# Where the attention output is split into 16-bit halves: at its making, or at its use by the output projection

## Chip, cores and metric

One core of one Trainium2 chip. The metric is the device time of one execution in microseconds (us); lower is better. TensorE is PE, VectorE DVE, ScalarE ACT, GpSimd POOL, and SyncE, which issues nearly all transfers, SP.

## The reference

Two layers over 16 meta tokens and 2048 frames of width 1024. Layer 0 (a linear recurrence and a state-space branch) isn't touched. Layer 1 is stick-breaking attention with 16 heads of 64, a gate, an output projection and a residual; a norm follows, and the meta tokens are dropped:

```
u = rmsnorm(h, norm_w)
q, k, v, g = split(u @ w_in, 4)
z = einsum('bthd,bshd->bhts', q, k) * 64 ** -0.5
log_keep = where(before, log_sigmoid(-z), 0)            # before: key index < query index
csum = cumsum(log_keep, axis=-1)
weights = where(before, exp(log_sigmoid(z) + csum[..., -1:] - csum), 0)
o = einsum('bhts,bshd->bthd', weights, v)
o = o * silu(g)
h = h + o @ w_out
return rmsnorm(h, final_norm)[:, 16:]
```

## The kernel before

Every product in float32 precision is made of three products of 16-bit halves (`mm3`, lines 395 to 397): each operand is written as a high and a low half, and high x high, high x low and low x high are summed.

**Stages.** Layer 0 fills the time to about 1400 us. Layer 1 follows and is written by a planner: `build_proj(p)` and `build_attn(p)` for eight pairs of heads, and `build_out()` at last, only list operations with an engine, a duration, a priority and the buffers they use. `Planner.run` lays them out once, always taking the operation that can start first by its own durations and, among those, the one of the smallest priority number. The order per engine is then fixed in the program: each engine runs its list from the front and waits at whatever isn't ready.

**Projection of a pair** (`build_proj`): keys, values, queries and gate, in chunks of up to 512 columns, each chunk 24 matmuls. The gate lands in `sg`, four buffers, one per 512 queries (L1875 on ACT, L1878 on DVE). The value path has a split of its own into halves: ACT copies to 16 bits (L1789), DVE subtracts (L1792), from SBUF to SBUF.

**Attention of a pair** (`build_attn`): four blocks `i` of 512 queries. For each block the key blocks go from the diagonal one down to the meta tokens. A *score step* is 128 queries against up to 512 keys for two heads: four matmuls into `zp` (L1911, two buffers), a sigmoid on ACT (L1934), two scans on DVE (L1939 on the diagonal, widths 128, 256, 384 and 512; L1942 elsewhere, width 512), a copy to 16 bits on ACT (L1946), the low half on POOL (L1949), and a transposing transfer into `tb` on SP (L1953). Four score steps make a *value step*: 24 matmuls into `op` (L1986). A block ends with a meta score step (16 narrow matmuls, scan L2010) and a meta matmul (L2032). Then its output is made: DVE scales it and adds a term into `og` (L2040), POOL multiplies it by the gate (L2043), and SP stores it as float32 into `o_d` (L2046): 32 such blocks, 8 pairs by 4.

**Output projection** (`build_out`): 16 tiles of 128 tokens, O0 to O15. A tile's load from `o_d` needs the block of all eight pairs, so O0 to O3 need the last pair's first block, O4 to O7 its second. The weights of `w_out` are split on ACT and DVE (L2104, L2107). For each tile SP loads float32 into `wraw` (two buffers, L2131), ACT makes the high half (L2134) and DVE the low half (L2137) in `ohl`, PE runs 48 matmuls in two column halves, DVE adds the residual (L2157), ACT squares and sums (L2161), and the norm follows (L2168 to L2177) with the store. The first six tiles share one `ohl` buffer, `first`; the later ones go round four.

Of the kernel before, what the change touches and what calls it, by code (L numbers as in the profile page):

```python
# [8 lines left out]
F32 = mybir.dt.float32  # L9
F32R = mybir.dt.float32r  # L10
F16 = mybir.dt.float16
I32 = mybir.dt.int32
U16 = mybir.dt.uint16
AF = mybir.ActivationFunctionType
# [5 lines left out]
P = 128  # L20
D = 1024
KT = 8
# [241 lines left out]
def trunk_kernel(ctx: ExitStack, tc: tile.TileContext, a: dict, out: bass.AP, stop=None):  # L264
# [26 lines left out]
    wz_d = dram.tile([3, P, 2, KT, 256], F16, name="wz_d")  # L291
    ac_d = dram.tile([HEADS, NT, P], F32, name="ac_d")
    h1_d = dram.tile([L, D], F32, name="h1_d")
    o_d = dram.tile([P, KT, SEQ], F32, name="o_d")

    ident = const.tile([P, P], F32, name="ident")
    make_identity(nc, ident)
# [1395 lines left out]
    def act_t(n, psum=True, ap=False):  # L1693
        return n * 0.000833 + 0.2 + (0.03 if ap else 0.0)

    def dve_t(n, ap=False):
        return n * 0.00104 + 0.068 + (0.06 if ap else 0.0)
# [187 lines left out]
    def build_attn(p):  # L1885
# [107 lines left out]
        def mstep(ui, prio):  # L1993
# [48 lines left out]
            def fg():  # L2042
                G.tensor_tensor(out=og.t, in0=og.t, in1=sg.t, op=ALU.mult)  # L2043

            def fd():
                nc.sync.dma_start(out=o_d[:, p, 512 * i:512 * i + 512], in_=og.t)  # L2046
            sd.op("V", dve_t(512), fo, r=[op, (vt, 0), (vt, 1), (vt, i + 1)], w=[og], prio=prio + PV_LAG)
            sd.op("G", gp_t(512), fg, r=[sg], w=[og], prio=prio + PV_LAG)
            sd.op(SP, DMA_T - 0.1, fd, r=[og], w=[(od_b, (p, i))], prio=prio + PV_LAG, lat=2.5)

        for ui, u in enumerate(units):
            t0 = start[ui]
# [13 lines left out]

    def build_out():
        base = TP * 8 + D_OFF
        oform = ("ohl", [P, 2, KT, P], F16)
        w1 = [sd.buf("u%d" % c, ("w1", [P, 2, 2, D], F16)) for c in range(4)]  # L2070
        w1r = sd.buf("vv", ("w1r", [P, 2, D], F32))
        slots = [(sd.buf("wraw", ("w1s", [P, 1, D], F32)), 0) for _ in range(6)] + [(w1r, 0), (w1r, 1)]
# [7 lines left out]
        def f1():  # L2080
            V.tensor_tensor(out=w1c[:, 0:KT], in0=osc, in1=w1m, op=ALU.mult)
            V.tensor_reduce(out=w1c[:, KT:KT + 1], in_=w1c[:, 0:KT], op=ALU.max, axis=AX.X)

        def f2():
            T.matmul(psc.t[:, 0:1], ones, w1c[:, KT:KT + 1], start=True, stop=True)
# [11 lines left out]
        for k, (b, o) in enumerate(slots):  # L2097
# [5 lines left out]
            def fh(k=k, b=b, o=o):  # L2103
                S.activation(out=wv(0, k), in_=b.t[:, o], func=AF.Copy, scale=w1c[:, k:k + 1])  # L2104

            def fl(k=k, b=b, o=o):
                V.scalar_tensor_tensor(out=wv(1, k), in0=b.t[:, o], scalar=w1c[:, k:k + 1], in1=wv(0, k),  # L2107
                                       op0=ALU.mult, op1=ALU.subtract)
# [11 lines left out]
        rest = [sd.buf(x, oform) for x in ("kk", "vv", "vv")] + [first]  # L2120
        for t in range(SEQ // P):
            pr = base - 50 + 11 * t
            raw, ohl = sd.buf("wraw"), first if t < D_TWO else rest[(t - D_TWO) % 4]
            hb, jk = [sd.buf(x, ("h1" + x, [P, 512], F32)) for x in ("whi", "wlo")], sd.buf("og", ("junk", [P, 2, 512], F16))
            st = {}

            def o3(ohl, i):
                return ohl.t[:, i]

            def ld1(t=t, raw=raw):  # L2130
                nc.sync.dma_start(out=raw.t, in_=o_d[:, :, P * t:P * t + P])  # L2131

            def fh(raw=raw, ohl=ohl):
                S.activation(out=o3(ohl, 0), in_=raw.t, func=AF.Copy)  # L2134

            def fl(raw=raw, ohl=ohl):
                V.tensor_tensor(out=o3(ohl, 1), in0=raw.t, in1=o3(ohl, 0), op=ALU.subtract)  # L2137
            sd.op(SP, DMA_T - 0.1, ld1, r=[(od_b, (p, t // 4)) for p in range(8)], w=[raw], prio=pr - 30, lat=3.5, rank=pr)
            for h in range(2):
                def ld2(t=t, b=hb[h], h=h):  # L2140
                    nc.sync.dma_start(out=b.t, in_=h1_d[NM + P * t:NM + P * t + P, 512 * h:512 * h + 512])
                sd.op(SP, DMA_T - 0.1, ld2, w=[hb[h]], prio=pr - 20, lat=3.0, rank=pr)
            sd.op("S", 0.95, fh, r=[raw], w=[(ohl, 0)], prio=pr - EVAC, rank=pr)
            sd.op("V", 1.13, fl, r=[raw, (ohl, 0)], w=[(ohl, 1)], prio=pr - EVAC)
            for h in range(2):
                hs = slice(512 * h, 512 * h + 512)
                ps = sd.buf("acc")
                for s0 in range(0, KT, 2):
                    def f(s0=s0, ps=ps, hs=hs, ohl=ohl):
                        mm3(ps.t, (lambda k: o3(ohl, 0)[:, s0 + k, :], lambda k: o3(ohl, 1)[:, s0 + k, :]),  # L2150
                            (lambda k: wv(0, s0 + k)[:, hs], lambda k: wv(1, s0 + k)[:, hs]), 2,
                            start=s0 == 0, stop=s0 == KT - 2)
                    sd.op("T", mmt(512, 6), f, w=[ps], prio=pr + D_MM + 5 * h + s0 * 0.5,
                          r=[(ohl, 0), (ohl, 1)] + [(w1[s0 // 2], (x, s0 + k)) for x in range(2) for k in range(2)])

                def fa(ps=ps, b=hb[h]):
                    V.scalar_tensor_tensor(out=b.t, in0=ps.t, scalar=w1c[:, KT + 1:KT + 2], in1=b.t, op0=ALU.mult, op1=ALU.add)  # L2157

                def fq(b=hb[h], jk=jk, h=h, st=st):
                    st["ss%d" % h] = small.tile([P, 1], F32, name="sse%d" % h)  # L2160
                    S.activation(out=jk.t[:, h], in_=b.t, func=AF.Square,  # L2161
                                 accum_out=st["ss%d" % h])
                sd.op("V", dve_t(512), fa, r=[ps], w=[hb[h]], prio=pr + 6 + 5 * h - EVAC)
                oq = sd.op("S", 0.6, fq, r=[hb[h]], w=[(jk, h)], prio=pr + 6 + 5 * h - EVAC)
# [56 lines left out]
```

## Time and profile before

| what | us |
|---|---|
| median of three runs (lowest, highest) | 2712.23 (2711.01, 2716.89) |
| the profiled execution | 2712.38 |
| its span | 2710.6 |
| PE busy in the span | 2618.6 (97%) |
| DVE busy | 2076.7 (77%) |
| ACT busy | 1645.0 (61%) |
| POOL busy | 1237.7 (46%) |

The span is what the trace covers; the execution's own time is 1.8 us longer. Times in the trace count from the span's start. A matmul's listed duration overlaps that of the next one, so what one costs is read from start to start. The granted clock of PE is given as a share of full speed: 1.00 is 2.4 GHz, and 0.5 would be 1.2 GHz.

### The profile page before, as it was taken

How to read it: one execution, taken by the hardware profiler on the slowest of the kernel's cores; microseconds unless marked ns; L12 is line 12 of the kernel's file. 1: busy time of each engine (PE TensorE's matmuls, PEld its weight loads, DVE VectorE, ACT ScalarE, POOL GpSimd, SP SyncE). 2: the span in 40 equal slices, each digit the busy share in tenths (PEclk: the TensorE clock that was granted, in tenths of full speed). 3: DMA queues.
4: the chain of work that ended last, by engine and by line, in shares of the span. 5: the costliest groups of instructions: out<-in, count | busy, mean ns of one | idle time of the engine just before them, and what ended most of it. 6: DMA issues, size and time to landing. Idle time of an engine off the chain costs nothing. (4 is left out here: it accounts for less than half of the span.)

```text
span 2710.6 us, 44621 instructions
## 1 busy us (share of the span) xinstructions
PE 2618.6 (97%) x16597; PEld 1406.4 (52%) x16597; DVE 2076.7 (77%) x2945; ACT 1645.0 (61%) x2516; POOL 1237.7 (46%) x1256
## 2 busy tenths in 40 slices
PE   7999999987999999999999999999999999999998
PEld 5765656564655555554454444444444444443344
DVE  8887786878564877689846888888888888888953
ACT  7756647456554666576625666676666666666621
POOL 4100100011203455456615776777676777766610
PEclk9999999998998999999999999999999999999999
DMA  8111111654325687888845788788787887789862
GB/s 226 53 51 55 32 55 47 196 189 136 115 98 131 176 194 177 192 184 180 182 103 118 164 175 169 171 161 175 154 179 162 169 173 163 178 170 221 211 186 101
DMA packets 974716, 404.87 MB, mean 149 GB/s; under 512 B 804017, under 2 KB 935681, under 8 KB 972834
## 3 DMA queue, kind: packets, MB, share of 16 engines
q1 hardware_dynamic: 967760, 385.39, 60.9%
q0 software_dynamic: 4640, 16.59, 1.6%
q8 instruction: 130, 2.13, 0.3%
q14 instruction: 88, 0.72, 0.1%
q10 hardware_dynamic: 2098, 0.05, 0.0%
HBM read 144.66 MB, written 60.22 MB: 76 GB/s over the span
## 5 line engine op out<-in xcount | busy, mean ns | idle before, releaser
L395 PE MATMUL acc<-u,whi 128*128 128x512 f16 (+4 forms) x2336 | 801.7, 344 | 2.9 <-DVE jk L670 1.5
L396 PE MATMUL acc<-u,whi 128*128 128x512 f16 (+4 forms) x2336 | 799.4, 343 | 2.4 <-DVE u L705 2.4
L397 PE MATMUL acc<-u,wlo 128*128 128x512 f16 (+4 forms) x2336 | 799.2, 343 | 0.0
L1949 POOL TENSOR_TENSOR hl<-e,hl 128x1024 f16<-128x1024 f32 (+2 forms) x320 | 602.5, 1886 | 187.1 <-ACT hl L1946 179.2
L1942 DVE TENSOR_TENSOR_SCAN e<-zp,carry,zero 128x512 f32<-128x512 f32 x384 | 470.6, 1267 | 47.4 <-ACT zp L1934 17.2
L1934 ACT ACTIVATE zp<-zp,ncz 128x1024 f32<-128x1024 f32 (+2 forms) x320 | 304.6, 956 | 197.4 <-PE zp L1911 166.0
L395 PEld LDWEIGHTS <-whi 128*128 128x128 f16 x2336 | 232.4, 99 | 208.6 <-issue 45.1
L1946 ACT ACTIVATE hl<-e 128x1024 f16<-128x1024 f32 (+2 forms) x320 | 293.9, 922 | 61.1 <-DVE e L1942 22.0
L397 PEld LDWEIGHTS <-wlo 128*128 128x128 f16 x2336 | 229.6, 98 | 195.1 <-issue 3.1
L396 PEld LDWEIGHTS <-whi 128*128 128x128 f16 x2336 | 229.8, 98 | 165.4 <-issue 2.4
L1911 PE MATMUL zp<-kk,qt 64*128 64x512 f16 (+9 forms) x1792 | 276.2, 301 | 7.5 <-DVE e L1939 4.5
L1939 DVE TENSOR_TENSOR_SCAN e<-zp,onehot 128x128 f32<-128x128 f32 (+3 forms) x256 | 195.6, 807 | 70.0 <-ACT zp L1934 33.4
L1911 PEld LDWEIGHTS <-qt 128*128 128x128 f16 (+1 forms) x1792 | 97.8, 95 | 192.1 <-issue 119.7
L1986 PE MATMUL op<-tb,vv 128*64 128x512 f16 (+3 forms) x1920 | 193.6, 351 | 0.5 <-DMA tb<-hl 0.2
L1986 PEld LDWEIGHTS <-vv 128*64 128x64 f16 x1920 | 101.0, 110 | 91.4 <-issue 27.8
L481 DVE SCALAR_TENSOR_TENSOR cv<-xin,scv,cv 128x512 f32<-128x512 f32 (+2 forms) x180 | 122.5, 695 | 10.6 <-ACT cv L479 8.3
L363 POOL TENSOR_TENSOR wraw<-wraw,gain 128x2048 f32<-128x2048 f32 (+1 forms) x9 | 33.4, 3706 | 172.0 <-DMA wraw<-in_even_w_in_dram 172.0
L1333 ACT ACTIVATE acr<-acr,act 128x128 f32<-128x128 f32 (+1 forms) x272 | 84.8, 382 | 38.8 <-DMA acr<-ac_d 36.9
L771 DVE SCALAR_TENSOR_TENSOR lx<-xin,prm,lx 128x512 f32<-128x512 f32 (+5 forms) x144 | 96.9, 679 | 11.3 <-ACT lx L757 7.7
L397 PE MATMUL acc<-w,ohl 128*128 128x512 f16 x256 | 98.3, 384 | 4.7 <-DVE ohl L2137 4.7
L395 PE MATMUL ops<-woh,ya 128*128 128x512 f16 x256 | 99.5, 389 | 0.4 <-DVE mb L978 0.3
L543 POOL TENSOR_TENSOR wraw<-wraw,gain 128x2048 f32<-128x2048 f32 x8 | 30.5, 3816 | 151.8 <-DMA wraw<-in_even_w_in_dram 134.7
(376 smaller groups left out, 5025.5 us busy)
## 6 DMA issues: line engine op xcount, KB each, us to landing
wraw<-in_even_w_in_dram SPq DMA_DIRECT2D x17, 1024.0 KB, 5.3
wr<-in_even_w_out_dram SPq DMA_DIRECT2D x32, 512.0 KB, 4.2
acr<-ac_d SPq DMA_DIRECT2D x64, 256.0 KB, 4.3
wraw<-in_odd_w_in_dram SPq DMA_DIRECT2D x30, 512.0 KB, 5.1
xh_d<-hw SPq DMA_DIRECT2D x20, 516.0 KB, 3.3
wz<-wz_d SPq DMA_DIRECT2D x9, 1024.0 KB, 5.4
ya_d<-ri POOLq DMA_DIRECT2D x16, 516.0 KB, 3.0
xt<-in_x_dram SPq DMA_DIRECT2D x16, 512.0 KB, 5.2
```

The lines of the kernel that those rows point to most:

```text
L395: T.matmul(ps, lh(k), rh(k), start=start and k == 0, stop=False)
L396: T.matmul(ps, lh(k), rl(k), start=False, stop=False)
L397: T.matmul(ps, ll(k), rh(k), start=False, stop=stop and k == nk - 1)
L481: V.scalar_tensor_tensor(out=dst[:, c0:c0 + n], in0=xin[:, j:j + n], scalar=wv[:, j:j + 1], in1=dst[:, c0:c0 + n], op0=ALU.mult, op1=ALU.add)
L771: V.scalar_tensor_tensor(out=lx.t[:, c0:c0 + n], in0=xin.t[:, q:q + n], scalar=prm[:, kt, q:q + 1], in1=lx.t[:, c0:c0 + n], op0=ALU.mult, ...
L1911: T.matmul(zp(hd), qt[rs, 2 if tl == ROWS else hd, P * j:P * j + P], k[rs, hd, ks], start=tl == order[0] and x == 0, stop=tl == order[1] a ...
L1934: S.activation(out=zp.t[:, :, :wd], in_=zp.t[:, :, :wd], func=AF.Sigmoid, scale=scl["ncz"])
L1939: V.tensor_tensor_scan(out=er, data0=kr, data1=onehot[:, 512 - wd:][:, ::-1], initial=0.0, op0=ALU.mult, op1=ALU.max)
L1942: V.tensor_tensor_scan(out=er, data0=kr, data1=zero.to_broadcast([P, wd]), initial=cin.t[:, 2 * j + hd:2 * j + hd + 1], op0=ALU.mult, op1= ...
L1946: S.activation(out=hlv()[:, :, 0], in_=ev(), func=AF.Copy)
L1949: (V if vl else G).tensor_tensor(out=hlv()[:, :, 1], in0=ev(), in1=hlv()[:, :, 0], op=ALU.subtract)
L1986: T.matmul(op.t[64 * hd:64 * hd + 64, c0:], vv.t[:, v0 + m, vi, 64 * hd:64 * hd + 64], tb.t[:, m, 2 * hd + wi, c0:], start=diag and m == 0 ...
```

## The change

`o_d` holds 16-bit halves instead of float32, in the same number of bytes: per partition and block of 128 tokens first the high, then the low half. The halves are made where the block's output is made: after POOL's gate product ACT copies `og` to 16 bits and DVE subtracts, both into the gate's buffer `sg`, whose bytes are free by then; SP stores from there. The output projection loads halves straight into `ohl`, and its two conversion passes per tile are gone. O0 to O5 now use the two `wraw` buffers as `ohl`, in place of the one `first`.

```
-    o_d = dram.tile([P, KT, SEQ], F32, name="o_d")
+    o_d = dram.tile([P, KT, SEQ // P, 2, P], F16, name="o_d")
...
+            o4 = lambda: og.t.rearrange("p (m c) -> p m c", c=P)
+            oh = lambda: sg.t.bitcast(F16).rearrange("p (m s c) -> p m s c", s=2, c=P)
+            def f1():
+                S.activation(out=oh()[:, :, 0], in_=o4(), func=AF.Copy)
+            def f2():
+                V.tensor_tensor(out=oh()[:, :, 1], in0=o4(), in1=oh()[:, :, 0], op=ALU.subtract)
             def fd():
-                nc.sync.dma_start(out=o_d[:, p, 512 * i:512 * i + 512], in_=og.t)
+                nc.sync.dma_start(out=o_d[:, p, 4 * i:4 * i + 4], in_=oh())
...
-            sd.op(SP, DMA_T - 0.1, fd, r=[og], w=[(od_b, (p, i))], prio=prio + PV_LAG, lat=2.5)
+            sd.op("S", act_t(512, psum=False), f1, r=[og], w=[sg], prio=prio + PV_LAG)
+            sd.op("V", dve_t(512), f2, r=[og], w=[sg], prio=prio + PV_LAG)
+            sd.op(SP, DMA_T - 0.1, fd, r=[sg], w=[(od_b, (p, i))], prio=prio + PV_LAG, lat=2.5)
...
-            raw, ohl = sd.buf("wraw"), first if t < D_TWO else rest[(t - D_TWO) % 4]
+            ohl = sd.buf("wraw", oform) if t < D_TWO else rest[(t - D_TWO) % 4]
...
-                nc.sync.dma_start(out=raw.t, in_=o_d[:, :, P * t:P * t + P])
+                nc.sync.dma_start(out=ohl.t, in_=o_d[:, :, t])
...
-            sd.op("S", 0.95, fh, r=[raw], w=[(ohl, 0)], prio=pr - EVAC, rank=pr)
-            sd.op("V", 1.13, fl, r=[raw, (ohl, 0)], w=[(ohl, 1)], prio=pr - EVAC)
```

Since the planner lays all of layer 1 out anew, the order of every engine changes from the first pair on. Two places matter for what follows. The first is DVE after the last gate chunk of the last pair (`sg<-acc`; scans stand as SCALAR_TENSOR_TENSOR with `e` as output; L2119 in the changed kernel is L2107 before, L2161 is L2157, and L2053 is the new subtraction). Before:

```order
L1878 SCALAR_TENSOR_TENSOR sg<-acc,co,sg 128x512
L1939 SCALAR_TENSOR_TENSOR e<-zp,onehot 128x384 x2
L2107 SCALAR_TENSOR_TENSOR w_26697<-w1r,w1c,w_26697 128x1024
L2137 TENSOR_TENSOR ohl<-wraw,ohl 128x1024
L1939 SCALAR_TENSOR_TENSOR e<-zp,onehot 128x512 x2
L2107 SCALAR_TENSOR_TENSOR w_26697<-w1r,w1c,w_26697 128x1024
L2040 SCALAR_TENSOR_TENSOR og<-op,vt 128x512
L1942 SCALAR_TENSOR_TENSOR e<-zp,carry,zero 128x512 x5
L2157 SCALAR_TENSOR_TENSOR h1whi<-acc,w1c,h1whi 128x512
```

And now:

```order
L1939 SCALAR_TENSOR_TENSOR e<-zp,onehot 128x256 x2
L2119 SCALAR_TENSOR_TENSOR w_26529<-w1r,w1c,w_26529 128x1024
L1939 SCALAR_TENSOR_TENSOR e<-zp,onehot 128x384 x2
L2119 SCALAR_TENSOR_TENSOR w_26529<-w1r,w1c,w_26529 128x1024
L1878 SCALAR_TENSOR_TENSOR sg<-acc,co,sg 128x512
L1939 SCALAR_TENSOR_TENSOR e<-zp,onehot 128x512 x2
L2040 SCALAR_TENSOR_TENSOR og<-op,vt 128x512
L1942 SCALAR_TENSOR_TENSOR e<-zp,carry,zero 128x512 x2
L2053 TENSOR_TENSOR sg<-og,sg 128x4x128
L1942 SCALAR_TENSOR_TENSOR e<-zp,carry,zero 128x512 x6
L1939 SCALAR_TENSOR_TENSOR e<-zp,onehot 128x128 x2
```

From the last gate chunk to the first residual add of O0 (L2157) stood five single scans of L1942; now eight stand there, and a further diagonal set begins before it.

The second place is SP around the store of the last pair's block and the first loads for the output projection (`tb<-hl` are the transposes, `o_d` the stores and loads). Before, the store and what follows it:

```order
L2046 DMA o_d<-og 128x512
L2101 DMA w1s<-in_odd_w_out_dram 128x1024
L1953 DMA_TRANSPOSE tb<-hl 128x16x128
L2101 DMA w1s<-in_odd_w_out_dram 128x1024
L1953 DMA_TRANSPOSE tb<-hl 128x16x128 x2
L2131 DMA wraw<-o_d 128x8x128 x2
L2141 DMA h1whi<-h_d 128x512
```

And now:

```order
L1953 DMA_TRANSPOSE tb<-hl 128x12x128
L2056 DMA o_d<-sg 128x1024
L1953 DMA_TRANSPOSE tb<-hl 128x16x128 x2
L2130 DMA sg<-in_final_norm_dram 128x512
L2143 DMA ohl<-o_d 128x8x256
L1953 DMA_TRANSPOSE tb<-hl 128x16x128
L2143 DMA ohl<-o_d 128x8x256
```

The first load of an output tile stood three transposes and two weight loads behind the store; now two transposes and the load of a gain stand between.

## Rows read from the trace of the kernel before

**Rows 1.** Busy by stretch: start:end, length, PE, PEld, DVE, ACT, POOL, clock, DMA

```profile
1500.00:2474.65 974.65, 971.50 (x6266) 450.78 (x6264) 814.29 (x1036) 652.46 (x837) 705.63 (x754) 1.00 0.82 172
2474.65:2489.35 14.70, 10.10 (x43) 3.45 (x42) 13.61 (x16) 10.46 (x15) 10.93 (x12) 0.65 0.93 198
2489.35:2590.60 101.25, 94.44 (x539) 38.34 (x538) 87.94 (x88) 59.88 (x79) 65.22 (x60) 0.97 0.90 212
2590.60:2703.30 112.70, 112.67 (x522) 50.88 (x520) 44.12 (x72) 24.25 (x51) 6.75 (x11) 1.00 0.42 138
```

**Rows 2.** Waits of PE, 2400 to 2711: us in total, times, longest

```profile
PE acc L397 <- DVE ohl L2137: 4.7, 2, 3.2
PE zp L1911 <- DVE e L1939: 4.4, 2, 2.9
PE zp L1911 <- DVE e L1942: 2.1, 3, 1.3
```

**Rows 3.** Timeline of PE: start, duration, instruction, [idle before, its releaser]

```profile
2468.26 0.55 PE L1911 MATMUL zp<-kk,qt 128*128 128x16 f16 x16
...
2474.43 0.38 PE L397 MATMUL acc<-u,wlo 128*128 128x512 f16 x1
...
2488.50 0.92 PE L1911 MATMUL zp<-kk,qt 128*128 128x512 f16 x4
2489.35 0.39 PE L395 MATMUL acc<-w,ohl 128*128 128x512 f16 x1
...
2510.36 0.39 PE L397 MATMUL acc<-w,ohl 128*128 128x512 f16 x1 [3.21 <-DVE ohl L2137]
```

**Rows 4.** Chain of work that ended last: start, duration

```profile
2587.57 2.71 PE op L1986 x24
2590.28 0.32 PE op L2032
...
2703.05 0.23 PE acc L397
```

**Rows 5.** Instructions on tile ohl: ns min/median/max, first and last start

```profile
L2134 ACT ACTIVATE ohl<-wraw x16: 1043/1057/1059, 2480.9 to 2661.6; 128x1024 f16<-128x1024 f32 x16
L2137 DVE TENSOR_TENSOR ohl<-wraw,ohl x16: 1203/1225/2923, 2482.9 to 2662.7; 128x1024 f16<-128x1024 f32 x16
```

**Rows 6.** Instructions on tile vs, the values' split

```profile
L1789 ACT ACTIVATE vs<-dv x40: 399/618/631, 1415.6 to 2410.9; 128x512 f16<-128x512 f32 x24, 128x256 f16<-128x256 f32 x16
```

**Rows 7.** DVE by line and shape, 1500 to 2450: busy us, mean ns

```profile
L1942 DVE TENSOR_TENSOR_SCAN e<-zp,carry,zero 128x512 f32<-128x512 f32 x325 | 398.2, 1267 | 37.6 <-ACT zp L1934 17.2 <-POOL hl L1949 11.1 <-issue 4.7
L1939 DVE TENSOR_TENSOR_SCAN e<-zp,onehot 128x512 f32<-128x512 f32 x53 | 62.5, 1208 | 8.0 <-ACT zp L1934 3.4 <-issue 1.8 <-POOL carry L1964 1.7
L1939 DVE TENSOR_TENSOR_SCAN e<-zp,onehot 128x384 f32<-128x384 f32 x54 | 48.8, 942 | 20.8 <-POOL em L2000 5.1 <-POOL hl L1949 4.3 <-issue 3.8
L1939 DVE TENSOR_TENSOR_SCAN e<-zp,onehot 128x256 f32<-128x256 f32 x54 | 34.4, 674 | 11.1 <-POOL hl L1949 6.8 <-issue 2.7 <-ACT zp L1934 1.5
L1792 DVE TENSOR_TENSOR vs<-dv,vs 128x512 f16<-128x512 f32 x21 | 25.4, 1209 | 3.4 <-ACT vs L1789 3.4
L1939 DVE TENSOR_TENSOR_SCAN e<-zp,onehot 128x128 f32<-128x128 f32 x54 | 19.9, 406 | 23.0 <-ACT zp L1934 21.6 <-POOL hl L1949 1.3
```

**Rows 8.** Instructions on tile og

```profile
L2040 DVE SCALAR_TENSOR_TENSOR og<-op,vt x32: 659/688/692, 1467.5 to 2590.7; 128x512 f32<-128x512 f32 x32
L2043 POOL TENSOR_TENSOR og<-og,sg x32: 1258/1269/1282, 1469.3 to 2591.5; 128x512 f32<-128x512 f32 x32
```

**Rows 9.** Busy times of ten microseconds around the wait in rows 3

```profile
2510.00:2520.00 10.00, 9.64 (x65) 3.80 (x66) 9.61 (x10) 3.79 (x5) 5.00 (x5) 0.83 0.86 216
```

**Rows 10.** Transfers: issuer, count, KB each, median us from issue to landing

```profile
o_d<-og SPq DMA_DIRECT2D x32, 256.0 KB, 2.5
wraw<-o_d SPq DMA_DIRECT2D x16, 512.0 KB, 4.5
```

**Rows 11.** Timeline of SP's queue: start, duration, instruction

```profile
2456.85 5.40 SPq L1953 DMA_TRANSPOSE tb<-hl  x2
```

More of the change, by code (lines that the diff above doesn't have):

```diff
@@ L2068, in build_out @@
         base = TP * 8 + D_OFF
-        oform = ("ohl", [P, 2, KT, P], F16)
+        oform = ("ohl", [P, KT, 2, P], F16)
         w1 = [sd.buf("u%d" % c, ("w1", [P, 2, 2, D], F16)) for c in range(4)]
@@ L2127, in o3, with ld1 @@
             def o3(ohl, i):
-                return ohl.t[:, i]
-            def ld1(t=t, raw=raw):
-                nc.sync.dma_start(out=raw.t, in_=o_d[:, :, P * t:P * t + P])
[L2133 to L2138, printed above, removed]
+                return ohl.t[:, :, i]
+            def ld1(t=t, ohl=ohl):
+                nc.sync.dma_start(out=ohl.t, in_=o_d[:, :, t])
+            sd.op(SP, DMA_T - 0.1, ld1, r=[(od_b, (p, t // 4)) for p in range(8)], w=[ohl], prio=pr - 30, lat=3.5, rank=pr)
             for h in range(2):
@@ L2153, in build_out @@
                     sd.op("T", mmt(512, 6), f, w=[ps], prio=pr + D_MM + 5 * h + s0 * 0.5,
-                          r=[(ohl, 0), (ohl, 1)] + [(w1[s0 // 2], (x, s0 + k)) for x in range(2) for k in range(2)])
+                          r=[ohl] + [(w1[s0 // 2], (x, s0 + k)) for x in range(2) for k in range(2)])
                 def fa(ps=ps, b=hb[h]):
```

## Prediction, made before the changed kernel was run

> **What bounds the kernel now.** I read the busy times by stretch first, then what TensorE (PE) waited for, then PE's timeline where it waits, then the chain at the end. From 1500 us to the end of the last projection matmul, PE is busy 971.50 of 974.65 us at full clock [rows 1]: attention there only paces itself, and projection matmuls of the next head pair fill every gap. Nothing that the change does there on VectorE (DVE), ScalarE (ACT) or GpSimd (POOL) can be repaid; it can only open a gap. After the last projection matmul three stretches follow. The reader should see in each how much of it is PE work:
>
> - The *gap*, 2474.65 to 2489.35: attention of the last pair runs with nothing beside it, since the first matmul of the output projection (call its token tiles O0 to O15) stands behind it. 14.70 us, DVE busy 13.61 of them, clock 0.65 [rows 1].
> - The *fill*, 2489.35 to 2590.60: O matmuls between attention steps. 101.25 us, DVE busy 87.94 [rows 1]. PE waits for DVE: 4.7 us for the converted halves (L2137), 2.1 for scans [rows 2].
> - The *drain*, 2590.60 to 2703.3: 522 O matmuls, PE busy 112.67 of 112.70 [rows 1]. 112.70/522 = 0.216 us per matmul. The conversions of the later tiles lie wholly under it.
>
> PE's work is the same in both kernels, so the time changes only by what PE loses to waiting and to a low clock. Its prices, from starts in the timeline: one step of four 512-column score matmuls 0.85 us (2488.50 to 2489.35) [rows 3]; a value step of 24 matmuls 2.71; the closing meta matmul 0.25, between the 0.32 of its row and one matmul's 0.216 [rows 4]; narrower steps by columns (a diagonal value step (512+384+256+128)/(4x512) of 2.71 = 1.7); a meta score step 0.55 [rows 3]. The gap holds one 384-column step, three 512, one full value step and a meta matmul: 0.64 + 2.55 + 2.71 + 0.25 = 6.15 us, so it loses 8.55. The fill holds 246 O matmuls (53.1), 19 full score steps (16.2), a narrow set (1.3), two meta score steps (1.1), five full and two diagonal value steps (17.0), two meta matmuls (0.5): 89.2. It loses 12.1: 6.8 idle (L2137 and L1942) [rows 2], some 3 by the clock (0.97 of 94.44) [rows 1], 2.5 in switches.
>
> **Removed and moved.** Sixteen ACT passes of 1.057 us and sixteen DVE passes of 1.225 (one took 2.923) [rows 5]; nine of each lie in the drain and are worth nothing. The seven before it are 8.6 + 1.7 = 10.3 us of DVE work where DVE is nearly full. With them goes a hand-over between the load of a tile and its matmuls, and two of the DVE waits: the 4.7 us, one of 3.21 [rows 2, 3].
>
> **Added.** Thirty-two ACT passes on 128x512 (nearest: the same copy to 16 bits for V, 0.618 [rows 6]) and thirty-two DVE subtractions. The nearest row for these is the V split, the same operation and shape in the same stage: mean 1.209 [rows 7]. The lower bound is half of L2137's median at double the width, 0.61 [rows 5]; the upper is 2.9, that row's longest. I take 1.2. I put the excess of 1.2 over 0.61 down to POOL, which is busy 705.63 of 974.65 us there [rows 1] and 6.75 of 112.70 in the drain, where L2137 runs at its median. The Trainium skill's page "SBUF — State Buffer", section "Who interferes with whom", says that a DVE instruction with two SBUF inputs contends with a GpSimd instruction that reads SBUF, and that one of them blocks until the other ends. The trace agrees as far as 1.209 against 0.61 goes. The rule speaks against this change: the subtraction leaves a stage without POOL work for one with it; by the row the cost to PE is the 1 us below, by that rule of the Trainium skill, taken to its end, it is rival 3.
>
> 28 of the 32 stand before the last pair's fill: 28 x 1.2 = 34 us on DVE (814.29 of 974.65 busy), 17 us on ACT (652.46) [rows 1]. They fit into idle time, so I cost them on PE at 1 us (0 to 4): PE lost 3.2 there although V's splits ran at twice 0.61.
>
> **What the order makes of it.** The planner, seeing busier engines, lets attention fall behind the projections. Counted in PE's written order, what stands before the last projection matmul lacks five 512-column score steps, one each of 384, 256 and 128, a meta score step, two diagonal value steps and a meta matmul: 4.25 + 1.27 + 0.55 + 3.4 + 0.25 = 9.7 us. So projection ends at 2474.65 - 9.7 + 1 = 2466.0, with more attention left.
>
> *The gap grows.* Before its first O matmul now stand: two 384 steps, five 512, 256 and 128, a meta score step, two diagonal value steps, one meta matmul: 1.28 + 4.25 + 0.64 + 0.55 + 3.4 + 0.25 = 10.4 us of PE. DVE sets the pace: a score tile has two buffers, so each step waits for the scans two steps earlier. By the changed DVE order (shown in front) the first O follows when these are done: pairs of scans at 128, 256, 384, 512 (0.81, 1.35, 1.88, 2.42), two weight splits (1.23 each, the shape of L2137), a gate (0.69, the shape of L2040), L2040 (0.69), a full pair (2.53), the new subtraction (1.2), three full pairs (7.6), 128 again (0.81) [rows 5, 7, 8]: 22.4, and one PE step 0.64. DVE is busy 93% of the present gap and 87% of the fill [rows 1]: 22.4/0.93 + 0.64 = 24.7, 22.4/0.87 + 0.64 = 26.4, and it may start up to 2 us after the projection's end. I take 25 by the gap, the nearer row, and keep 22 (no idle, part done early) to 30. First O at 2491.0, loss 25 - 10.4 = 14.6: **+6.1** against 8.55.
>
> *The fill loses less.* It now holds 300 O matmuls (64.8), 22 full score steps (18.7), the narrow set and meta steps (2.4), six full and two diagonal value steps (19.7), three meta matmuls (0.75): 106.3. DVE's share: 87.9 + three more steps 7.6 - six L2137 9.0 + two subtractions 2.4 + a tile's four more passes 2.8 = 91.7. Now 87.9 stand against 89.2 on PE; then 91.7 against 106.3, so PE leads. The 4.7 us on L2137 go, and most of the clock's 3 with them (the clock read 0.83 after that wait [rows 9]); the scan waits may rise by 1. I take a loss of 6, between 2 (the switches alone) and 12.1 (what is late next takes all): **-6.1**. It ends at 2491.0 + 112.3 = 2603.3.
>
> *The drain* is shorter by the 54 matmuls that went into the fill: 468 x 0.216 = 101.1. PE ends at 2704.4 against 2703.3.
>
> *Costed at nothing.* Store and load keep their bytes, and runs of 2 KB and 512 B. A load lands in 4.5 us, a store in 2.5 [rows 10]. Tiles 0 to 5 now land in two buffers that are free only after a tile's matmuls: 4.5 against the next tile's 48 x 0.216 = 10.4, cover 5.9; if SP's queue is later than that, the rest is a wait. The gate's buffer is held for a store longer; the next pair fills it a pair's time later. The chain at the end keeps its shape.
>
> **Sum.** 1 + 6.1 - 6.1 + 0 = +1 on 2712.38, the profiled execution's own time (0.15 above the median): **2713**.
>
> **Rivals.**
>
> 1. *Faster: DVE is the bound after the projection and simply sheds work.* For it: 13.61 of 14.70 busy, the waits on L2137. Against it: the three extra steps in the gap. Gap 22 instead of 25, fill loss 2, dense stretch 0: -1 - 3 - 4 = -8 from the forecast: 2705.
>
> 2. *Slower: the new hand-overs replace the removed one.* The store for O0 now waits L2040 0.69, POOL's gate product 1.27, the ACT pass 0.62, the subtraction 1.2, then 2.5 to land; behind the store on SP stand two transposes (5.40 for two that wait [rows 11]) and only then the load, 4.5 [rows 6, 8, 10, 11]. That is 10.8 to 16.2, with queueing on ACT and POOL 13 to 20, from L2040, which starts 9.6 to 12 us after the projection's end. It decides from about 15 upward; at 20 the first O is at 32 instead of 25: +7, and a transpose held behind the waiting store costs the next scans a us: 2721. For it: the changed SP order puts the store before those transposes. Against it: the DVE order leaves six scans between.
>
> 3. *Slower: the subtraction's waits beside POOL break the written order.* The planner lays 0.6 out for each; if the unplanned 0.6 of 28 reaches PE undiminished, that is +17: 2729. The rule of the Trainium skill quoted above would give this result. Against it: V's splits exceed their plan as much, and PE lost only 3.2 us in 974.65.
>
> **How the numbers follow.** Forecast (within 0.2%, 2707 to 2717.8, which is about what a measurement of this kernel can tell from no change) 0.50; rival 1 0.24; rival 2 0.19; rival 3 0.07. The bounds of the terms run from -7 (dense 0, gap 22, fill 2, against forecast terms) to +15. For 8 in 10 I take 2703 to 2724: that leaves out rival 3 and the outer parts of the first two. Faster 0.24, same 0.50, slower 0.26.
>
> **What would show it.** Projection's last matmul near 2466; first O near 2491; the gap's PE busy near half; no PE wait for any half of O but perhaps for its load; last meta matmul near 2603; a drain without idle of some 101 us. Subtractions averaging 1.2 us before 2590. A first O before 2487 speaks for rival 1, one after 2495 with PE waiting on the load for rival 2, over 6 us of PE waits before 2466 for rival 3. I am wrong if the fill loses as much as before for a reason other than L2137, or if the dense stretch opens.

## The result, and where the time went

The changed kernel takes 2735.74 us in the median of 6 runs (2731.49 to 2739.16), the kernel before 2713.74 (6 runs beside it): ratio 1.008 [1.007, 1.0089]. The prediction was 2713, so 23 us were missed. The profiled execution of after spans 2731.9 us.

Busy times of after by the same stretches as [rows 1] (start:end, length, PE, PEld, DVE, ACT, POOL, clock, DMA):

```profile
1500.00:2484.00 984.00, 965.64 (x6159) 445.65 (x6157) 830.93 (x1045) 652.92 (x846) 699.47 (x736) 1.00 0.78 166
2484.00:2510.10 26.10, 15.87 (x102) 5.68 (x101) 22.76 (x28) 17.58 (x21) 17.25 (x19) 0.66 0.81 186
2510.10:2623.40 113.30, 108.84 (x630) 46.07 (x629) 88.59 (x95) 62.88 (x88) 70.20 (x71) 0.99 0.99 219
2623.40:2724.50 101.10, 101.10 (x469) 45.69 (x467) 31.09 (x57) 14.36 (x39) 6.19 (x10) 1.00 0.42 140
```

The projections end at 2484.0 instead of the predicted 2466.0. The gap (26.1 against 25), the fill (113.3 against 112.3) and the drain (101.1 against 101.1) came as predicted. So the miss lies in the first row: PE is idle 18.4 us of 984.0 where it was idle 3.2 of 974.7, although 9.7 us of attention had left the stretch.

To compare kernels whose orders differ I use one number for each stretch, the **loss**: its length, less the PE work in it, which is the matmuls of PE's written order at the prediction's prices (0.216, 0.85, 2.71, 0.55, 0.25 us). The dense stretch is the one up to the last projection matmul, and for this number it starts at the first score matmul of layer 1. The work of the whole is 1219.7 us in every kernel. The prices carry an error of their own, so differences count and not the 18.8. A loss is read from one profiled execution. It leaves out layer 0, which no edit touches: layer 1 starts between 1437.2 and 1446.0 us in these traces, and this accounts for much of what separates a profiled execution from its kernel's median.

| | dense: length, work, loss | gap loss | fill loss | sum of losses |
|---|---|---|---|---|
| before | 1030.5 - 1011.7 = 18.8 | 8.6 | 12.0 | 39.4 |
| after | 1040.8 - 1002.0 = 38.8 | 15.8 | 7.0 | 61.6 |

Of the +22, 20.0 are the dense stretch. Some 15.2 of them are idle time of PE (18.4 against 3.2). Another 3.4, an estimate from the rows, are clock: before had a granted clock of 1.00 throughout this stretch, while after was granted about 0.50 (1.2 GHz) from 1697.0 to 1700.4 us and from 2113.4 to 2116.8, after PE had waited 1.99 and 1.78 us for a scan. The first of the two waits, and the stretch behind it:

```profile
1696.24 0.95 PE L1911 MATMUL zp<-kk,qt 128*128 128x512 f16 x4 [1.99 <-DVE e L1942]
```

```profile
1697.00:1700.40 3.40, 3.40 (x10) 1.19 (x9) 3.40 (x5) 2.06 (x2) 1.87 (x5) 0.50 1.15 254
```

What PE, and the queue of SP, waited for in after from 1440 to 2480 us (total, times, longest; PEld is PE's loading of weights, and its waits overlap PE's own, so the two don't add):

```profile
PEld L1911 <- DVE e L1942: 16.7, 18, 2.5
PEld L1911 <- DVE e L1939: 10.9, 12, 2.3
PE zp L1911 <- DVE e L1942: 9.2, 9, 2.0
PE zp L1911 <- DVE e L1939: 5.9, 7, 1.8
PE acc L1210 <- DVE wm L1196: 3.0, 4, 1.0
```

```profile
SPq L2056 <- DVE sg L2053: 26.5, 10, 4.6
```

PE's score matmuls wait for DVE's scans. Before, all of PE's waits in the dense stretch came to 2.8 us, 0.6 of them for scans:

```profile
PE acc L1210 <- DVE wm L1196: 2.0, 2, 1.0
PE zp L1911 <- DVE e L1942: 0.4, 2, 0.3
PE op L1986 <- issue: 0.2, 1, 0.2
PE zp L1911 <- DVE e L1939: 0.2, 1, 0.2
```

And SP's queue stands 26.5 us before the store L2056, because the subtraction L2053 isn't done. The store of before waited 5.1 us in all in the same stretch, for POOL; the longest of these waits, and the one for the gate product itself, were these. A wait in SP's queue is no cost by itself, though: SP of before also stood 31.0 us ahead of the transposes of V, for V's split, while PE lost next to nothing.

```profile
SPq L2046 <- POOL inj L1968: 2.0, 1, 2.0
SPq L2046 <- POOL og L2043: 0.4, 1, 0.4
SPq L1795 <- DVE vs L1792: 31.0, 11, 5.0
```

One place where PE waits so, in the timeline of after (start, duration, engine, instruction, [idle before, its releaser]):

```profile
2418.71 3.88 SPq L1953 DMA_TRANSPOSE tb<-hl  x2
...
2421.66 0.63 ACT L2050 ACTIVATE sg<-og 128x512 f16<-128x512 f32 x1
...
2422.70 2.12 POOL L1949 TENSOR_TENSOR hl<-e,hl 128x1024 f16<-128x1024 f32 x1
...
2422.88 2.50 DVE L2053 TENSOR_TENSOR sg<-og,sg 128x512 f16<-128x512 f32 x1
...
2425.38 2.58 POOL L1949 TENSOR_TENSOR hl<-e,hl 128x1024 f16<-128x1024 f32 x1
2425.40 0.33 SPq L2056 DMA_DIRECT2D o_d<-sg  x1
...
2426.00 1.24 SPq L1795 DMA_TRANSPOSE vv<-vs  x1
...
2426.46 1.53 DVE L2103 TENSOR_SCALAR w1c<-osc,w1c 128x8 f32<-128x8 f32 x1
...
2427.33 4.06 SPq L1953 DMA_TRANSPOSE tb<-hl  x2
...
2427.97 2.44 DVE L1942 TENSOR_TENSOR_SCAN e<-zp,carry,zero 128x512 f32<-128x512 f32 x2
...
2430.47 0.93 PE L1911 MATMUL zp<-kk,qt 128*128 128x512 f16 x4 [1.82 <-DVE e L1942]
```

The subtraction starts 0.18 us after POOL's low half and takes 2.50 us where it can take 0.67. SP is done with its transposes at 2422.59 and then stands 2.8 us, until 2425.40, before the store; two kinds of transposes queue behind it. The scans of DVE come last, and PE waits 1.82 us. Both delays, of DVE and of SP, start at one instruction; the experiments take them apart as far as they can be.

### The profile page after: what moved, and what is told of

Read it like the earlier page. It is cut to its first block, busy times and chain, and to the rows that moved or that the text cites. A ratio compares the mean times of both kernels' runs of the same rounds, so it can differ in the third digit from the quotient of the medians.

```text
span 2731.9 us, 44582 instructions
## 1 busy us (share of the span) xinstructions
PE 2619.0 (96%) x16597; PEld 1407.0 (52%) x16597; DVE 2091.3 (77%) x2961; ACT 1648.1 (60%) x2532; POOL 1244.9 (46%) x1256
## 5 line engine op out<-in xcount | busy, mean ns | idle before, releaser
L1942 DVE TENSOR_TENSOR_SCAN e<-zp,carry,zero 128x512 f32<-128x512 f32 x384 | 469.6, 1265 | 52.4 <-ACT zp L1934 25.8
L1911 PE MATMUL zp<-kk,qt 128*128 128x512 f16 (+9 forms) x1792 | 277.0, 302 | 26.1 <-DVE e L1942 13.8
L771 DVE SCALAR_TENSOR_TENSOR lx<-xin,prm,lx 128x512 f32<-128x512 f32 (+5 forms) x144 | 97.0, 679 | 11.4 <-ACT lx L757 7.7
L395 PE MATMUL ops<-woh,yb 128*128 128x512 f16 x256 | 98.3, 384 | 0.8 <-DMA yb<-hl 0.8
```

The costliest lines, as they stand in the source:

```text
L395: T.matmul(ps, lh(k), rh(k), start=start and k == 0, stop=False)
L771: V.scalar_tensor_tensor(out=lx.t[:, c0:c0 + n], in0=xin.t[:, q:q + n], scalar=prm[:, kt, q:q + 1], in1=lx.t[:, c0:c0 + n], op0=ALU.mult, ...
L1911: T.matmul(zp(hd), qt[rs, 2 if tl == ROWS else hd, P * j:P * j + P], k[rs, hd, ks], start=tl == order[0] and x == 0, stop=tl == order[1] a ...
L1942: V.tensor_tensor_scan(out=er, data0=kr, data1=zero.to_broadcast([P, wd]), initial=cin.t[:, 2 * j + hd:2 * j + hd + 1], op0=ALU.mult, op1= ...
```

## Experiments

Three theories: **W**, DVE's own time on the subtractions beside POOL's work; **H**, the hand-over, that is the store that waits for the subtraction ahead of transposes in SP's queue; **O** (L in some expectations), the planner's other order, whatever is in it. Losses as above; work in brackets only where it matters.

**Passes and planning, each alone**

e1_unplanned: both passes planned at no cost, so that the planner keeps before's balance between projections and attention.

```
-sd.op("S", act_t(512, psum=False), f1, ...)
-sd.op("V", dve_t(512), f2, ...)
+sd.op("S", 0.0, f1, ...)
+sd.op("V", 0.0, f2, ...)
```

> The changed kernel, but the planner is told that the two new passes take no time (0.0 in place of 0.63 and 0.60 us); the same instructions run. Theory W (the passes' own time beside POOL opens the waits before the projection's end): the order is tighter still and the passes last as long, so as slow as the changed kernel or slower, 2735 to 2750. Theory O (the planner's reaction, another order with attention further behind, opens them): the order comes back near that of the kernel before, and the time to 2712 to 2722.

Measured: 1.0064 [1.0047, 1.0081]; losses 48.3, 3.2, 8.7 (dense, gap, fill). The worst dense stretch of all: a plan that doesn't know the passes makes this stretch worse. The time, 2730, lies in neither range; the gap loses 3.2 where after's lost 15.8.

e2_nosplit: no passes. POOL writes the gate product as the 16-bit high half, which is stored; the low halves are zeros (left out).

```
-G.tensor_tensor(out=og.t, in0=og.t, in1=sg.t, op=ALU.mult)
+G.tensor_tensor(out=og2, in0=og.t, in1=sg.t, op=ALU.mult)
-sd.op("S", ..., f1, ...); sd.op("V", ..., f2, ...)
-nc.sync.dma_start(out=o_d[:, p, 4 * i:4 * i + 4], in_=oh())
+nc.sync.dma_start(out=o_d[:, p, 4 * i:4 * i + 4, 0], in_=og2...)
```

> The changed kernel without the two passes: POOL's gate product is written as the 16-bit high half at once and stored alone (256-byte runs); the low halves are zeros, written once by 16 small stores. It leaves out the low half of the attention output. Output projection as in the changed kernel: it loads halves and converts nothing. Theory W: without the passes the dense stretch closes (PE waits there 3 us as before) and the shed conversions show alone: 2700 to 2712. Theory O: another new order, so anywhere between 2705 and 2735, with PE waits in the dense stretch of up to 15 us.

Measured: 0.9953 [0.9938, 0.9968]; losses 19.5, 3.2, 5.6. The time, 2699.5, is just under W's range. PE's work in each stretch is e1's (1011.7, 1.5, 105.4, 101.1 in both), though not its order, so the passes with what waits for them, and with the order that the planner then writes, cost 28.8 us in e1's dense stretch and 3.1 in its fill. It also shows what the removed half of the change is worth: gap and fill lose 11.8 us less than before.

e5_before_plus: the kernel before with both passes added and planned, their result unused, the store as before.

```
 sd.op("G", gp_t(512), fg, r=[sg], w=[og], ...)
+sd.op("S", act_t(512, psum=False), f1, r=[og], w=[sg], ...)
+sd.op("V", dve_t(512), f2, r=[og], w=[sg], ...)
```

> The kernel before with the two passes added where the changed kernel has them, into the gate's buffer, planned at the same times; nobody reads them, the float32 store and the conversions at the output projection stay. Theory W: all the loss without the gain, PE waits of 15 us or more before the projection's end, 2735 to 2745. Theory O: an order of its own again, 2712 to 2740, and its PE waits before the projection's end need not be near the changed kernel's.

Measured: 1.0031 [1.0017, 1.0044]; losses 26.3, 11.8, 14.6. The passes without the waiting store cost 7.5 in the dense stretch, not 20; W alone had said 15 us of waits and 2735 or more, and both were missed.

**Is it the luck of one order?** Any edit makes the planner rewrite the order. Four kernels change only one planned duration: p_b1 (`SCAN_F` 0.13 to 0.132, in before), p_b2 (`G_F` 0.15 to 0.152, before), p_b3 (`SCAN_F` to 0.128, before); p_a1 and p_a3 are `SCAN_F` 0.132 and 0.128 in after.

> The kernel before, computing the same, with one planner constant moved by 0.002 us (a scan is planned at 1.289 in place of 1.287 us): no instruction is added or lengthened, only the order is laid out anew. Theory W: within 0.3% of the kernel before, 2706 to 2721. Theory O: orders differ by as much as the change did, so 2712 to 2740, with PE waits before the projection's end of 8 us or more.

> The kernel before, nothing of the change, with one number of the planner changed (the fixed part of GpSimd's and of such steps' planned time, 0.150 to 0.152 us). Nothing else is computed or moved; PE's written order differs from before's in 3456 rows of a line-by-line difference, from row 20277. Loss is the length of the dense stretch less the priced PE work in it (before 18.8 us). Theory L, before's order is a rare good one and any rewriting of it loses several us in the dense stretch: loss 24 to 34, time 2716 to 2730. Theory W and H, only the added work and its hand-overs open it: loss 17 to 22, time 2708 to 2715.

> As p_b2 with another number (the fixed part of a scan's planned time 0.130 to 0.128 us): 4616 rows of the difference, from row 20037. L: loss 24 to 34, time 2716 to 2730. W and H: loss 17 to 22, time 2708 to 2715.

> The changed kernel with the scan's planned fixed part 0.130 to 0.132 us: 4716 rows of PE's order differ from the changed kernel's, from row 21190. The changed kernel's dense loss was 38.8. If its 20 us over before come from the passes and hand-overs (W, H), the loss stays at 33 to 45, time 2728 to 2742. If they are a matter of one unlucky order (L), it scatters: below 30 in one of p_a1 and p_a3 at least.

> The changed kernel with the scan's planned fixed part 0.130 to 0.128 us: 6068 rows differ from the changed kernel's, from row 18337. W, H: loss 33 to 45, time 2728 to 2742. L: it scatters, below 30 in one of p_a1 and p_a3 at least.

| | ratio | dense loss | gap | fill | PE's waits for scans, dense |
|---|---|---|---|---|---|
| p_b1 | 1.0003 [0.9992, 1.0013] | 18.9 | 7.7 | 12.3 | 0.4 |
| p_b2 | 1.0016 [1.0006, 1.0025] | 21.5 | 3.5 | 20.2 | 0.2 |
| p_b3 | 1.0031 [1.0019, 1.0042] | 22.1 | 6.0 | 18.8 | 2.1 |
| p_a1 | 1.0065 [1.005, 1.008] | 36.4 | 15.2 | 6.6 | 15.2 |
| p_a3 | 1.0047 [1.0032, 1.0062] | 33.2 | 11.4 | 10.1 | 8.9 |

Before's orders lose 18.8 to 22.1 in the dense stretch, after's 33.2 to 38.8: the loss belongs to the change, by some 11 at the nearest pair and 20 at the widest. PE's waits for scans say the same (0.6 in before, 15.1 in after). But an order alone is worth 3 to 6 us there, and up to 0.3% of the time: by its time p_b3 fell into L's range, and p_a1 and p_a3 stayed below W's and H's. (p_b1 changes few rows of the order only; it says little.) The length of the store's wait is not its price either. In p_a3 SP stood longest, and lost least of the three:

```profile
SPq L2056 <- DVE sg L2053: 40.8, 16, 4.6
```

**Which of the added things?** All four start from e2_nosplit and are planned at 0.0.

r1_sub: only the 32 subtractions, nobody waits for them.

```
+V.tensor_tensor(out=oh()[:, :, 1], in0=o4(), in1=og2..., op=ALU.subtract)
+sd.op("V", 0.0, f2, r=[og, og2_b], w=[sg], ...)
```

> The kernel without the two passes (its dense stretch, from the first score matmul of layer 1 to the last projection matmul, took 1031.2 us, PE waits 3.5 in it, time 2699.5), with the 32 subtractions alone put back on DVE, at 0.0 in the plan, their result used by nobody; the store waits for the gate product alone, as without them. So PE's order is nearly that of the kernel without passes and SP queues behind nothing new. (The store carries the high half only: the low one is zeros.) Theory W, DVE's own time beside POOL opens PE's waits: dense 1036 to 1046, PE waits 7 to 15, time 2705 to 2715. Theory H, it is the store that waits for the passes, in SP's queue ahead of transposes: dense 1030 to 1033, 2697 to 2703. Theory O, the planner's reaction: as H.

Measured: 1.0013 [1.0003, 1.0022]; losses 30.5, 3.2, 9.9. W holds for 11.0 us in the dense stretch, and this is the cleanest pair of all: the written orders of PE, ACT and POOL are e2's, row for row. PE's waits for scans rise from 0.7 to 9.4.

r5_store: as r1_sub, and the store carries the subtraction's result (the high half is left out).

```
-..., in_=og2...)           # r=[og2_b]
+..., in_=oh()[:, :, 1])    # r=[sg]
```

> r1_sub, but the store carries the subtraction's result and so waits for it on SP (same bytes as in r1_sub; the high half is left out instead of the low one). W: as r1_sub, within 3 us. H: dense 1040 to 1050, 8 or more above r1_sub, time 2710 to 2722. O: as r1_sub.

Measured: 1.0039 [1.0025, 1.0052]; losses 39.5, 2.9, 8.6, 9.0 more than r1_sub in the dense stretch. SP waits 23.1 us for the subtraction. It came as H said, but the pair isn't clean: the planner, told that the store waits, wrote another order of PE, and the 9.0 holds that too. That order is e1's, row for row, so e1's further 8.8 (48.3) go with what else e1 has: ACT's pass, its hand-overs, and both halves in the store.

r3_act: only ACT's pass; POOL writes f32 in place, the store waits for ACT.

```
-G.tensor_tensor(out=og2, ...)
+G.tensor_tensor(out=og.t, ...)
+S.activation(out=og2..., in_=o4(), func=AF.Copy)
```

> The kernel without the two passes, with the ACT pass alone put back: POOL writes the gate product in f32 in place, ACT makes the 16-bit half, the store waits for ACT; planned at 0.0. (High half only.) W: ACT does not contend with POOL, dense 1030 to 1033, time 2698 to 2703. H: the store now waits some 2 us more on SP, dense 1033 to 1038, 2702 to 2708. O: as without passes, 2697 to 2703.

Measured: 1.001 [0.9998, 1.0021]; losses 29.8, 6.7, 6.1. A miss for all three theories: 10 us in the dense stretch without any work on DVE. Its order differs from e2's in thousands of PE's rows. SP stands 12.1 us before the store for ACT's pass, so H may have a share in it; PE's waits for scans are 4.2.

r4_one: as r1_sub, with a step that reads one SBUF operand.

```
-V.tensor_tensor(out=oh()[:, :, 1], in0=o4(), in1=og2..., op=ALU.subtract)
+V.tensor_scalar(out=oh()[:, :, 1], in0=o4(), scalar1=1.0, scalar2=1.0, op0=ALU.mult, op1=ALU.mult)
```

> r1_sub with the subtraction replaced by a DVE step that reads one SBUF operand instead of two (the f32 product times 1.0 times 1.0, written to the same place; nobody uses it, the low half of the output is left out as there). Everything else, the written order too, is r1_sub's. r1_sub's dense loss (length less priced PE work) was 30.5 against 19.5 without the step. Theory W2, it is the waiting for POOL that a second SBUF operand brings: the step takes 0.4 to 0.75 us on average, dense loss 19 to 24, time 2698 to 2706. Theory W1, any added DVE step of about that size does it: loss 27 to 33, time 2707 to 2715.

Measured: 1.0001 [0.9991, 1.001]; losses 25.9, 5.0, 9.2. The dense loss lies between the two ranges: it doesn't decide. The step's times beside those of the subtraction, in r1_sub, r4_one, after and e10_poollate (below), in this order (ns min/median/max):

```profile
L2055 DVE TENSOR_TENSOR sg<-og,og x32: 666/1356/2598, 1467.7 to 2604.7; 128x512 f16<-128x512 f32 x32
```

```profile
L2055 DVE TENSOR_SCALAR sg<-og x32: 401/1248/2330, 1469.4 to 2602.9; 128x512 f16<-128x512 f32 x32
```

```profile
L2053 DVE TENSOR_TENSOR sg<-og,sg x32: 665/1120/2611, 1470.6 to 2626.8; 128x512 f16<-128x512 f32 x32
```

```profile
L2053 POOL TENSOR_TENSOR sg<-og,sg x32: 1150/1156/1465, 1472.1 to 2598.3; 128x512 f16<-128x512 f32 x32
```

The step with one operand is stretched too, from 0.40 to a median of 1.25, so it was no step free of POOL. The Trainium skill's page "SBUF — State Buffer", section "Who interferes with whom", says that such a step (tensor_scalar) can run in a mode that takes the ports shared with GpSimd and can then contend with it; my expectation overlooked that, and the stretched step agrees. How much of W is the waiting and how much the plain time stays open.

e8_order: the planner reserves the time and the hand-overs of both passes, but nothing is issued for them.

```
-sd.op("S", act_t(512, psum=False), f1, ...); sd.op("V", dve_t(512), f2, ...)
+sd.op("S", act_t(512, psum=False), lambda: None, ...); sd.op("V", dve_t(512), lambda: None, ...)
```

> The order of the changed kernel without its passes: the planner is told of an ACT and a DVE step of the same planned length and the same hand-overs, but nothing is issued for them, and POOL's product is written as the high half and stored. (Low half left out.) O, the planner's other order loses the time: dense 1038 to 1045 with 26 us of gap, time 2725 to 2735. W and H, the passes lose it: dense 1020 to 1025 (the 9.7 us of attention that were moved behind it are gone), gap 22 to 27, time 2710 to 2717.

Measured: 1.003 [1.0019, 1.0041]; losses 33.4, 7.3, 9.0. In the dense stretch as O said (14 without any pass), in the total between the two. The trace shows where half of the 14 lies (4.0, and some 3.4 by the clock): PE stands 4.02 us before a value step, for a release that the profile doesn't name, while one transpose holds SP's queue for 6.49 us, and then runs at a granted clock of 0.50:

```profile
2458.77 6.49 SPq L1955 DMA_TRANSPOSE tb<-hl  x1
...
2467.39 3.41 PE L1988 MATMUL op<-tb,vv 128*64 128x512 f16 x24 [4.02 <-issue]
```

```profile
2466.30:2473.10 6.80, 5.71 (x30) 3.05 (x31) 1.73 (x2) 1.82 (x2) 1.77 (x2) 0.50 0.98 255
```

After has no such place. PE's waits for scans, the greater part of after's loss, are 5.4 here against 15.1. Nor is it after's order: it holds 1007.9 us of PE work in the dense stretch, after's 1002.0. So e8_order shows that an order can lose this much by itself, and not that after's does. Why the planner's order has this place I didn't find.

**Taking the causes away, in kernels that compute all**

e9_late: one word. The planner believes that the subtraction's result comes 6 us later, and so writes the store further back in SP's order.

```
-sd.op("V", dve_t(512), f2, r=[og], w=[sg], prio=prio + PV_LAG)
+sd.op("V", dve_t(512), f2, r=[og], w=[sg], prio=prio + PV_LAG, lat=6.0)
```

> The changed kernel with the planner told that the subtraction's result is there 6 us later, so that it writes the store further back in SP's order, behind transposes that it now stands ahead of; both passes as they are. Dense loss of the changed kernel 38.8 (36.4 and 33.2 under two small changes of the planner's numbers). Theory H, the store's wait on SP holds up transposes: SP's wait for the subtraction falls from 26.5 us to under 12, dense loss 26 to 31, time 2721 to 2729. Theory W alone: loss 33 to 40, time 2728 to 2738.

Measured: 1.0006 [0.9997, 1.0016]; losses 26.4, 8.4, 8.0. No wait of the store for the subtraction is left, and the dense loss is 12.4 lower, as H had said. The planner rewrote PE's order with it, so the 12.4 hold an order too. The time is 9 us below H's range, since the rewritten plan also leaves less attention for the gap (work 7.0, loss 8.4). Its dense stretch, where the subtractions run as slowly as in after (mean 1.27 us against 1.29), has PE idle 8.9 instead of 18.4:

```profile
1500.00:2483.20 983.20, 974.29 (x6268) 449.85 (x6267) 846.53 (x1067) 670.43 (x868) 720.80 (x755) 1.00 0.81 170
```

e13_v_late: the same word in e1_unplanned, as a second pair.

> e1_unplanned (both passes planned at 0.0, so that the projections are not ahead of attention; dense loss 48.3, the largest seen, SP's waits for the subtraction 31.8 us) with the subtraction's result planned 6 us later, as in e9_late: a second pair of kernels that differ by the store's place in SP's order. The store's place (H): dense loss 26 to 34, time 2708 to 2718. If e9_late's gain was a matter of its particular order: 40 to 50, time 2722 to 2732.

Measured: 1.006 [1.0041, 1.0078]; losses 39.0, 4.0, 15.3. The dense loss falls by 9.3, from 48.3, and SP's 31.8 us of waits go; but it stays at 39, not at 26 to 34. The fill loses 6.6 more, and the time, 2725, lies in the range of the rival: against e1's 1.0064 it hasn't moved clear of noise. As a second pair it supports H in the dense stretch alone. With the pass planned at 0.0, DVE now stands before the subtraction until ACT has made the high half:

```profile
DVE sg L2053 <- ACT sg L2050: 14.4, 9, 2.2
```

In e1 that was 5.6 us, in e9 2.3. A wait seems to have moved from one queue to another.

e10_poollate: e9_late with the subtraction on POOL.

```
-V.tensor_tensor(out=oh()[:, :, 1], ...)    # sd.op("V", dve_t(512), ...)
+G.tensor_tensor(out=oh()[:, :, 1], ...)    # sd.op("G", gp_t(512), ...)
```

> e9_late with the subtraction moved from DVE to POOL, planned at POOL's price. DVE then has no added step; POOL has 28 more of some 1.3 us before the end of the projections. W and H together explain the loss: dense loss 20 to 27, time 2711 to 2722. If the planner's reaction or ACT's pass do (as r3_act and e8_order hint): 28 to 35, time 2722 to 2732.

Measured: 1.0008 [0.9997, 1.002]; losses 21.0, 16.7, 5.9. The dense loss is that of before's orders, with all passes made. PE idles 5.8 us of 973.8, while POOL carries 726.62:

```profile
1500.00:2473.80 973.80, 968.04 (x6226) 448.31 (x6224) 824.57 (x1033) 665.81 (x861) 726.62 (x777) 1.00 0.79 170
```

What keeps it at before's time is the gap: this plan leaves 10.2 us of PE's attention work there, before's 6.1.

e11_half: the change for tokens 0 to 1023 alone; the other blocks are stored in f32 and split after the load, as before.

```
+if i < 2:  # passes f1, f2 and the store of halves; else: store og.t to o_f
+if t >= 8: # load f32, split as in the kernel before
```

> The change made for tokens 0 to 1023 alone (O0 to O7, all that are multiplied before the drain); the other half of the attention output is stored in f32 and split after its load, as before, under the drain. 14 of the 28 added subtractions are gone from the dense stretch. If the loss goes with the number of passes: dense loss 26 to 31, gap and fill lose together 15 to 25, drain without idle, time 2718 to 2727. If one other order costs it whatever the number: 33 to 40, time 2726 to 2736.

Measured: 1.0029 [1.0018, 1.0041]; losses 31.0, 7.9, 9.4. With half of the passes the dense loss above before is 12.2 instead of 20.0.

e14_pool: e10_poollate with ACT's pass planned at 0.0, which brings the gap's work down to 1.5 us.

```
-sd.op("S", act_t(512, psum=False), f1, ...)
+sd.op("S", 0.0, f1, ...)
```

> The whole change with both cures and the small gap: subtraction on POOL, planned at POOL's price, its result planned 6 us later, ACT's pass planned at 0.0, which leaves as little attention after the projections as in the kernel without passes. If the dense loss is that of e10_poollate (21.0) and gap and fill lose what they did without passes (3.2 and 5.6, with passes 3 and 9): 1219.7 + 33 to 36 in layer 1 against 1219.7 + 39.3 before, time 2703 to 2708, ratio 0.997 to 0.999. If POOL's 28 steps hold up the scans' weights, dense loss 28 to 35: 2711 to 2720.

Measured: 0.9997 [0.9988, 1.0007]; losses 25.0, 4.3, 9.3, sum 38.6 against before's 39.4. The time, 2710, and the dense loss lie between the two ranges. It makes good all that the change lost and wins nothing: the gap's 4.3 and the fill's 2.7 less are spent on 6.2 more in the dense stretch.

**What is settled.** The 20 us are lost in the dense stretch, in all three orders of the change as it stands (33 to 39 against before's 19 to 22), and there mostly in waits of PE for scans. The subtractions on DVE are one cause, shown by adding them alone under one order (r1_sub, +11.0). **What is likely:** the place of the store that waits. Adding its wait lost 9.0 more (r5_store), and writing it later took 12.4 and 9.3 off (e9_late, e13_v_late). But each of these also rewrote PE's order, which alone is worth 3 to 6 us, the time of e13_v_late hardly moved, and p_a3 lost least with the longest wait. Moving the subtraction to POOL (e10_poollate, a further -5.4) lies within the same 3 to 6. **What is open:** r3_act's 10 and the 8.8 of e1_unplanned above r5_store; half of e8_order's 14; and the share of DVE's waiting for POOL in the 11. All single effects add to more than the whole, so they aren't independent.

## Why the prediction was wrong, step by step

- **The dense stretch (+1, 0 to 4): wrong, +20.** The step that failed is "They fit into idle time, so I cost them on PE at 1 us (0 to 4): PE lost 3.2 there although V's splits ran at twice 0.61." DVE's idle time there, 160 of 974.65 us [rows 1], is not slack: PE's next score matmul waits for one certain scan, and a subtraction written just ahead of it delays that scan however much DVE idles elsewhere. The splits of V, as long and as stretched, lose next to nothing in before, and the prediction took the new steps to be like them. Why they differ isn't shown: after's order was planned with its passes, just as before's with V's splits. r1_sub, whose subtractions nobody waits for, has the number that belongs in the place of the 1: 11.0. The subtractions' duration was nearly as predicted: 1.2 taken; in after from 1460 to 2460 it is this (busy us, mean ns):

```profile
L2053 DVE TENSOR_TENSOR sg<-og,sg 128x512 f16<-128x512 f32 x27 | 34.7, 1286 | 3.7 <-ACT sg L2050 3.6
```

  So the duration was right and its price on PE was not.
- **"Over 6 us of PE waits before 2466 speaks for rival 3": it spoke.** They are 18.1. Rival 3 had the place and nearly the size (17, 2729 us), but with a chance of 0.07. That its size came so near is in part luck: r1_sub gives 11.0 to the subtractions, and the waiting store, which rival 3 leaves out, is the likeliest candidate for the rest.
- **Hand-overs (rival 2).** I traced the store's wait, with transposes behind it, for O0 alone and priced it there. The same store stands in SP's queue 27 times before the gap, and waits there at 10 of them, 26.5 us. That term was put at nothing; what it costs PE is likely the rest beside the 11.0, as said above. For O0 the store did wait, 3.8 us, in the gap. The first load of halves is issued at 2502.9 and the first O follows at 2510.1, with no wait of PE right before it; the gap is 26.1, near the 25 of the forecast and not rival 2's 32. The store's wait in the gap, then the loads, issue and landing:

```profile
SPq L2056 <- DVE sg L2053: 3.8, 1, 3.8
```

```profile
L2143 SPq DMA_DIRECT2D ohl<-o_d x16: 527/549/656, 2502.9 to 2683.1; - x16
...
DMA to landing us min/median/max: 4.0/4.4/5.7
```

- **The gap: right.** Predicted loss 14.6, measured 15.8 (work 10.3). Its clock is 0.66, DVE is busy 22.76 of 26.10, 87%.
- **The fill: right.** Predicted loss 6, measured 7.0; no wait for halves is left, the clock is 0.99 where it was 0.97. From 2484 on PE waited for this:

```profile
PE zp L1911 <- DVE e L1939: 6.1, 5, 3.2
PE zp L1911 <- DVE e L1942: 4.5, 3, 2.4
PE op L1986 <- DMA tb<-hl: 3.6, 2, 2.7
```

- **The drain: right**, 101.1, without idle. **ACT and POOL: right** as durations, by the tile `og` of after, beside [rows 6, 8]:

```profile
L2043 POOL TENSOR_TENSOR og<-og,sg x32: 1262/1270/1641, 1468.4 to 2624.4; 128x512 f32<-128x512 f32 x32
L2050 ACT ACTIVATE sg<-og x32: 612/627/637, 1469.7 to 2625.7; 128x512 f16<-128x512 f32 x32
```

- **Rival 1** (DVE sheds work, -8) is real but hidden: with the passes away, e2_nosplit wins 11. The passes take it back and more.

The sum with the measured terms: +20.0 + 7.2 - 5.0 + 0 = +22.2 against the forecast's +1; layer 1 began 1.0 earlier, so the span grew by 21.3. The range had left out what it knew as rival 3.

## What to carry to other kernels

In a stretch where PE runs without idle time in a written order, idle time of the engine that feeds it is no free room for a new step: here 29 added subtractions (40.2 us of DVE in r1_sub) cost PE 11.0. Take the range from nothing to the whole duration until a run shows the price, and give the dear case a chance to match. Follow every added hand-over through the in-order queue in which the last of its chain waits, at each of its places and not only where the result is needed; planning the waiting store later (one planned latency) brought the whole change back to before's time, and moving the arithmetic as well won nothing more. A plan that changes rewrites the order, and the order alone moved this kernel by up to 0.3%: compare several orders of both kernels before a cause is named.

## What the runs showed of the hardware

DVE and POOL don't share the delay evenly here. The same subtraction takes 0.67 to 2.61 us on DVE and 1.15 to 1.47 on POOL. DVE's short steps wait as well as its long ones: a TENSOR_SCALAR on 8 columns took 1.53 us and ended at 2427.99, with the POOL instruction beside it (2425.38 + 2.58 = 2427.96, timeline above), while the same step took 0.23 in e10_poollate. A one-operand step on 512 columns took 0.40 to 2.33. So in these rows such a step's time depends less on its size than on what POOL does beside it.
